# Both branch projections in half products: Strassen units for the first branch, direct halves of the second parked in DRAM

## The chip, the cores and the metric

One core of one Trainium2 chip runs the kernel. The metric is the device time of one execution in microseconds (us), smaller being better. The five engines of the core run side by side, each with its own queue that it works off in order: PE multiplies matrices into PSUM, DVE (VectorE), ACT (ScalarE) and POOL (GpSimd) work element by element, and SP mostly issues DMAs, which move tiles between DRAM and SBUF. ACT issues DMAs too. Semaphores hold an instruction back until what it needs is there.

## The reference, cut to what matters

One layer of a streaming encoder for 1024 prompt rows and 128 sample rows, 1152 rows in all, of width 1024. Two branches make y_m (1152 x 2048) and y_a (1152 x 1024). The change touches only what comes after them:

```python
gate_m = jax.nn.sigmoid(mg_m + b_merge[:D_MODEL])
gate_a = jax.nn.sigmoid(mg_a + b_merge[D_MODEL:])
u = gate_m * jnp.einsum('ble,ed->bld', y_m, w_br_m) + gate_a * jnp.einsum('ble,ed->bld', y_a, w_br_a)
out = jnp.einsum('bld,de->ble', u, w_out)
x_new = layer_norm(DN_ALPHA * x + out, ln_g, ln_b)
```

So there are three products: y_m with w_br_m (2048 rows of weights), y_a with w_br_a (1024), and u with w_out (1024).

## The kernel before, in words

Every float32 number is split into a high part and a low part, and each product is three matmuls: high by high, high by low, low by high. The halving costs an ACT cast (the high part) and a DVE or POOL subtraction (the low part) for every operand. The 1152 columns (tokens) go in three chunks c of 384, which are `ch(0)` to `ch(2)`; the 1024 output channels in eight tiles j of 128. `acc` holds the projected sum, eight tiles by three chunks, in SBUF. `gate_d` in DRAM holds tanh values for the gates, j for the first branch and 8 + j for the second; (1 + tanh) stands for twice the sigmoid, and the factor 0.5 is put into w_out when it is split.

The end of the kernel is a row of stages, each of which keeps PE in one kind of product.

1. `quarter(A0)` multiplies 512 rows of w_br_m directly: four weight tiles, each with two j and three c, four row tiles k, three matmuls each, 288 matmuls. Each result is copied into `acc` by ACT.
2. `unit()` does the middle 1024 rows of w_br_m. For the columns of chunks 0 and 1 it uses Strassen's scheme (in Winograd's form): seven half products in place of eight; chunk 2 is done directly. It goes in four passes p, each for two output tiles j1, j2. A pass has eight weight pieces (B11, B21, B12, B22 and the differences T1 to T4) in an order that `PIECES` gives, and 11 products of 12 matmuls each: 528 in all. `prepare()` makes the piece three places ahead: for a T piece a subtraction first, then an ACT cast and a POOL subtraction. After each product `to()` adds the PSUM result into one to four places of `acc`, on DVE.
3. `quarter(A1)` does the last 512 rows of w_br_m directly; its evacuation `evac_m` adds the result to `acc` and multiplies by the first gate, on DVE.
4. `whole(B1s)` does the second branch, all 1024 rows of w_br_a directly, 576 matmuls. `evac_a` multiplies the result by the second gate on DVE and adds it to `acc` on POOL. Meanwhile `load_wo` loads and splits six of the eight row tiles of w_out; the last two come through the common weight stream (`todo`, `fetch`, `split`).
5. The output product goes chunk by chunk: `acc` is split into u's high and low parts, then 8 row tiles of w_out are multiplied, in chunk 0 with the row tile as the outer loop over six PSUM banks, and a layer norm on DVE follows. Each row tile of chunk 0 is 18 matmuls of 512 columns.

The inputs of the unit (sums and differences of row tiles of y_m) are made in `load_sums` while `quarter(A0)` runs, and the rows of `A1` in `rows_c01` and `rows_c2` while the unit runs. `Flow` meters these generators: a `yield n` gives way for n ticks, and a tick is six matmuls, about 1.04 us.

What sets the order: code inside `with tc.manual_schedule():` (the unit is one such section) goes to each engine's queue as written. Outside, a planner orders the instructions by program order and its own idea of when each becomes ready; `tc.high_priority(6000)`, used for the weight halving in `split()`, moves instructions up there. PSUM has eight banks, taken in turn by `bank()`. Buffers come by tag from pools: a new tile of a tag waits until the old one's readers are done. `wr` has one buffer for a raw weight tile, `wh` and `wl` two each for halves or pieces, `yr` four for row tiles.

## Time and profile before

| | |
|---|---|
| median of 3 runs | 2016.03 us (2015.63 to 2016.05) |
| profiled execution, its own time | 2015.91 us |
| its span, first to last instruction | 2014.1 us |
| PE busy | 2004.5 us of the span |
| DVE busy | 1299.2 us |
| ACT busy | 913.8 us |
| POOL busy | 531.4 us |
| DMA | 292.51 MB, mean 145 GB/s |

The profile page gives busy times of the engines, the chain of work that ended last, and groups of instructions. A group's row has line, engine, operation, out<-in, shape and count, then busy time and mean time of one instruction in ns, then the idle time before them and what ended it. A row of the timeline has start in us, duration in us, engine, line, operation and operands. A row of a windows view has the stretch, its length, busy time and instruction count of PE, weight loading, DVE, ACT and POOL, then the granted PE clock, the busy share of the DMA engines and GB/s. Times in views count from the start of the span. Matmuls overlap in the pipeline: the duration of one is longer than the distance from one start to the next.

### The profile page before, as it was taken

The numbers are of one execution on the slowest core, as the hardware profiler recorded it, in microseconds if no ns is written. First come the engines' busy times: TensorE is split into PE (matmuls) and PEld (weight loads), VectorE is DVE, ScalarE is ACT, GpSimd is POOL, SyncE is SP. The second block draws the span as 40 slices with busy tenths as digits, with TensorE's granted clock in tenths as the row PEclk, the third lists the DMA queues.
The fourth block names the chain that finished last, engine by engine and source line by source line (L and its number), as shares of the span: only waits on it lengthen the run. The fifth ranks groups of instructions, "written<-read, shape, count | busy, mean of one in ns | idle before, by whom it ended". The sixth has DMA issues, their size and how long they took to land.

```text
span 2014.1 us, 36174 instructions
## 1 busy us (share of the span) xinstructions
PE 2004.5 (100%) x14247; PEld 1861.9 (92%) x14247; DVE 1299.2 (65%) x2165; ACT 913.8 (45%) x1971; POOL 531.4 (26%) x708
## 2 busy tenths in 40 slices
PE   9999999999999999999999999999999999999998
PEld 7899999999999999999988988888989899999987
DVE  4145766666667676653577786787776787582355
ACT  4225555554655556543545546455455453221210
POOL 0012445354535354523001001100100005414400
PEclk9999999999999999999999999999999999999999
DMA  7422242424243323243566566566556662274322
GB/s 224 160 74 90 67 145 68 134 79 132 78 126 94 127 78 133 88 143 106 177 216 202 184 209 198 176 208 210 190 198 195 231 231 100 83 234 136 99 90 95
DMA packets 123626, 292.51 MB, mean 145 GB/s; under 512 B 18632, under 2 KB 74944, under 8 KB 113216
## 3 DMA queue, kind: packets, MB, share of 16 engines
q1 hardware_dynamic: 110480, 208.34, 32.3%
q10 hardware_dynamic: 12976, 81.86, 11.9%
q8 instruction: 112, 1.84, 0.4%
q14 instruction: 58, 0.48, 0.1%
HBM read 233.64 MB, written 56.51 MB: 144 GB/s over the span
## 4 chain that ended last, share of the span: by engine, by line
PE 90%; DVE 5%; DMA 2%; ACT 1%; issue 1%; POOL 0%; SPq 0%; ACTq 0%; DVEq 0%; POOLq 0%
PE d L245 19%; PE d L247 18%; PE d L246 18%; PE s L951 3%; PE o L1026 2%; PE y L736 2%; PE dq L245 2%; PE dq L246 2%; PE dq L247 2%; PE out L1614 2%; PE out L1613 2%; PE out L1615 2%; PE v L334 2%; PE v L333 2%; PE v L335 2%; PE so L1101 1%
## 5 line engine op out<-in xcount | busy, mean ns | idle before, releaser
L245 PE MATMUL d<-xh,wh 128*128 128x384 f32 x2112 | 736.1, 349 | 0.0
L247 PE MATMUL d<-xh,wl 128*128 128x384 f32 x2112 | 708.3, 335 | 0.0
L246 PE MATMUL d<-xl,wh 128*128 128x384 f32 x2112 | 707.2, 335 | 0.0
L245 PEld LDWEIGHTS d<-xh,wh 128*128 128x128 f32 x2112 | 396.6, 188 | 19.0 <-issue 8.1
L246 PEld LDWEIGHTS d<-xl,wh 128*128 128x128 f32 x2112 | 397.2, 188 | 0.8
L247 PEld LDWEIGHTS d<-xh,wl 128*128 128x128 f32 x2112 | 396.4, 188 | 0.0
L225 POOL TENSOR_TENSOR wl<-wr,wh 128x1024 fp32r<-128x1024 f32 x45 | 107.8, 2396 | 203.6 <-ACT wh L224 203.4
L956 ACT ACTIVATE st<-s,ckt 128x256 f32<-128x256 f32 (+1 forms) x320 | 115.1, 467 | 18.2 <-PE s L951 16.0
L224 ACT CAST wh<-wr 128x1024 fp32r<-128x1024 f32 x56 | 58.7, 1049 | 120.4 <-PE d L246 93.6
L1016 ACT ACTIVATE st<-st 128x1024 f32<-128x1024 f32 x80 | 83.2, 1062 | 40.9 <-DVE st L1011 38.0
L960 POOL TENSOR_TENSOR st<-st,mask_bf 128x256 f32<-128x256 f32 x64 | 49.7, 797 | 193.7 <-ACT st L956 193.4
L705 ACT ACTIVATE m<-ce,nacum 128x128 f32<-128x128 f32 x288 | 96.9, 392 | 5.7 <-PE y L736 5.7
L228 DVE SCALAR_TENSOR_TENSOR wl<-wr,wh 128x1024 fp32r<-128x1024 f32 x50 | 62.7, 1255 | 32.8 <-ACT wh L227 32.8
L1428 POOL TENSOR_TENSOR pc<-wu,pc 128x512 fp32r<-128x512 f32 x32 | 44.3, 1398 | 124.4 <-ACT pc L1427 124.3
L632 POOL TENSOR_TENSOR wx<-xdt,wdt 128x256 f32<-128x256 f32 x72 | 54.0, 752 | 84.8 <-DVE xdt L630 84.8
L1026 PE MATMUL o<-st,vt 128*64 128x256 f32 (+1 forms) x640 | 68.6, 363 | 0.2
L1026 PEld LDWEIGHTS o<-st,vt 128*64 128x64 f32 x640 | 43.0, 137 | 26.0 <-issue 3.0
L245 PE MATMUL d<-yb1h,wh 128*128 128x384 f32 x192 | 64.1, 334 | 0.0
L246 PE MATMUL d<-yb1l,wh 128*128 128x384 f32 x192 | 64.1, 334 | 0.0
L247 PE MATMUL d<-yb1h,wl 128*128 128x384 f32 x192 | 64.1, 334 | 0.0
L227 ACT ACTIVATE wh<-wr 128x1024 fp32r<-128x1024 f32 x50 | 52.7, 1054 | 22.2 <-PE d L246 22.2
L851 ACT ACTIVATE gate<-d,bcol 128x384 f32<-128x384 f32 x48 | 27.7, 578 | 71.8 <-PE d L247 46.6
(773 smaller groups left out, 4173.3 us busy)
## 6 DMA issues: line engine op xcount, KB each, us to landing
wr<-in_wt SPq DMA_DIRECT2D x88, 512.0 KB
kc<-in_cache_k ACTq DMA_DIRECT2D x32, 1024.0 KB
vc<-in_cache_v ACTq DMA_DIRECT2D x32, 1024.0 KB
ce<-ac_d SPq DMA_DIRECT2D x96, 192.0 KB
sb<-cs_d ACTq DMA_DIRECT2D x16, 576.0 KB
yr<-ym_d SPq DMA_DIRECT2D x16, 576.0 KB
g<-gate_d SPq DMA_DIRECT2D x48, 192.0 KB
gate_d<-gate SPq DMA_DIRECT2D x45, 192.0 KB
```

The source lines that it names most:

```text
L224: ac.copy(hi[:, :cols], raw[:, :cols])
L225: lazy.get("sub", po).tensor_tensor(lo[:, :cols], raw[:, :cols], hi[:, :cols].bitcast(F32), ALU.subtract)
L228: ve.scalar_tensor_tensor(lo[:, :cols], raw[:, :cols], scale, hi[:, :cols].bitcast(F32), ALU.mult, ALU.subtract)
L245: te.matmul(out, wh, xh, start=(k == 0), stop=False)
L246: te.matmul(out, wh, xl, start=False, stop=False)
L247: te.matmul(out, wl, xh, start=False, stop=(k == n - 1))
L632: po.tensor_tensor(wx[b][:], xdt[b][:], wdt[:, b, hs][:, :, None].to_broadcast([P, 4, 64]), ALU.mult)
L705: ac.activation(m[:, j, :], ce[:, j * P:(j + 1) * P], AF.Abs, bias=nacum[:, b, h:h + 1])
L951: te.matmul(ps2[:, e, 256 * x + q0:256 * x + 256], kk[hr, ks], qq[hr, qs], start=(at == 0), stop=(at == 2))
L956: ac.activation(S[j][:, e, kb, q0:], ps2[:, e, 256 * x + q0:256 * x + 256], AF.Identity, bias=ckt[:, kb, 2 * hp + e:2 * hp + e + 1])
L1016: ac.activation(w, w, AF.Exp, scale=-1.0)
L1026: te.matmul(o[64 * e:64 * e + 64, 256 * at + q0:256 * at + 256], vt[:, kb, 64 * e:64 * e + 64], S[j][:, e, kb, q0:256], start=(kb == 0), s ...
```

## The change

The second branch no longer has a stage of its own. Its 1024 rows of weights are cut into two direct halves of 512 rows, and these take the places of the two quarters of the first branch. The first branch is done wholly in two Strassen units of 1024 rows each. The order is: direct half of y_a, unit 0 (row tiles 4 to 11 of y_m), direct half of y_a, unit 1 (row tiles 0 to 3 and 12 to 15).

- The results of the direct halves can't stay in `acc`, which now belongs to the first branch. They go to a new DRAM tile `pa_d`: the first half through `acc` (ACT copies, then an ACT-queue DMA per j), the second through two small `gt` buffers (a copy and a DMA per j and c).
- `load_sums(v)` runs behind each direct half. Half of its S4 sums stay in the row buffer instead of a `gt` tile, and `gt` has two buffers instead of four, with a new tag `s4` of two.
- Unit 0 copies its first result into each place of `acc` with ACT, where all later ones are added by DVE.
- In unit 1 everything that the last two stages did on the way is put between the products, by `steps_1`: `seconds` loads both halves of the second branch and their gate for chunks 0 and 1, adds and gates them (two DVE instructions over 768 columns per j, three DMAs); `final` loads the first gate, `finish` applies it (DVE) and adds the second branch (POOL). For chunk 0 of the last two tiles this comes after piece T4 in pass 3, with the piece order of that pass changed; there, too, u's parts for chunk 0 are made (`parts_of_u`), and `load_wo` loads row tiles of w_out.
- Chunk 2 is finished during the output product by `late`, one j at a time, with four loads per j through the four small buffers.
- The row tiles of w_out are used in the order 0 to 7. Tiles 0 and 1 come from the weight stream: 0 is fetched at the sixth piece of pass 3 and split at the eighth, and the split then fetches tile 1 into the same raw buffer. `split_wo(k)` does tiles 2 to 7.

The diff, cut:

```diff
-    todo += [(I["wbr"][i], None, 1024) for i in range(12, 24)]
+    todo += [(I["wbr"][i], None, 1024) for i in range(12, 16)] + [None]
     todo += [(I["w_out"][k], 0.5, 1024) for k in range(2)]
...
+    ROWS = [range(4, 12), (0, 1, 2, 3, 12, 13, 14, 15)]
...
-            s4.append(mp.tile([P, CW], F32, tag="gt", name=f"s4_{i}", bufs=4))
-            ve.tensor_tensor(s4[i][:], y1[:, c0], y0[:, c0], ALU.subtract)
+            if i < 2:
+                s4[i] = mp.tile([P, CW], F32, tag="s4", name=f"s4_{v}{i}", bufs=2)[:]
+                ve.tensor_tensor(s4[i], y1[:, c0], y0[:, c0], ALU.subtract)
+            else:
+                s4[i] = y1[:, c0]
...
-    PIECES = [("B11", "B21", "B12", "B22", "T1", "T2", "T4", "T3")] + 3 * [("B11", "B21", "T1", "T2", "T4", "B12", "B22", "T3")]
+    ORDERS = (("B11", "B21", "B12", "B22", "T1", "T2", "T4", "T3"), ("B11", "B21", "T1", "T2", "T4", "B12", "B22", "T3"),
+              ("B11", "B21", "T1", "T2", "B12", "B22", "T4", "T3"))
+    PIECES = [ORDERS[i] for i in (0, 1, 1, 1, 0, 1, 1, 2)]
...
         def to(j, c, d):
-            ve.tensor_tensor(acc[:, j, ch(c)], acc[:, j, ch(c)], d, ALU.add)
-
+            a = acc[:, j, ch(c)]
+            if v == 0 and (j, c) not in begun:
+                begun.add((j, c))
+                ac.copy(a, d)
+            else:
+                ve.tensor_tensor(a, a, d, ALU.add)
...
-            for piece in PIECES[p]:
+            for at, piece in enumerate(order):
                 prepare()
                 if p == 3:
-                    if piece == "B12":
+                    if at == 5:
                         fetch()
-                    if piece == "T3":
+                    if at == 7:
                         split()
-                        flow.after(1, rows_c2)
...
+                steps(p, piece)
...
+    def evac_0(j, c, d):
+        ac.copy(acc[:, j, ch(c)], d)
+        if c == 2:
+            ac.dma_start(pa_d[0, j], acc[:, j, :])
...
+    def evac_1(j, c, d):
+        t = mp.tile([P, CW], F32, tag="gt", name=f"pa{j}_{c}", bufs=2)
+        ac.copy(t[:], d)
+        ac.dma_start(pa_d[1, j][:, ch(c)], t[:])
+
+    flow.start(load_sums(1))
+    quarter(A1, evac_1, lambda: unit_first(1))
+    flow.drain()
...
+    def seconds(*ps):
+
+        for j in (j for p in ps for j in (2 * p, 2 * p + 1)):
...
+            sy.dma_start(g, pa_d[0, j][:, 0:2 * CW])
+            sy.dma_start(x, pa_d[1, j][:, 0:2 * CW])
+            sy.dma_start(t, gate_d[8 + j][:, 0:2 * CW])
+            yield 5
+            ve.tensor_tensor(g, g, x, ALU.add)
+            yield 2
+            ve.scalar_tensor_tensor(g, t, 1.0, g, ALU.add, ALU.mult)
+            yield 1
...
+            ve.scalar_tensor_tensor(a, t[:], 1.0, a, ALU.add, ALU.mult)
+            po.tensor_tensor(a, a, G[j][:, ch(c)], ALU.add)
...
+    def late(j):
+
+        x0, x1, ta, tm = (pending.pop(0) for _ in range(4))
+        a = acc[:, j, ch(2)]
+        ve.tensor_tensor(x0, x0, x1, ALU.add)
+        ve.scalar_tensor_tensor(x0, ta, 1.0, x0, ALU.add, ALU.mult)
+        ve.scalar_tensor_tensor(a, tm, 1.0, a, ALU.add, ALU.mult)
+        po.tensor_tensor(a, a, x0, ALU.add)
+        if j < 7:
+            load_late(j + 1)
...
+    def parts_of_u(c, ks):
...
+        for k in ks:
+            ac.copy(h[:, k, :], acc[:, k, ch(c)])
+            ve.tensor_tensor(l[:, k, :], acc[:, k, ch(c)], h[:, k, :].bitcast(F32), ALU.subtract)
...
+    def steps_1(p, piece):
+
+        a, b = 2 * p, 2 * p + 1
+        at = PIECES[4 + p].index(piece)
+        if p:
+            if 1 <= at < 4:
+                finish(1)
+            if at < 4:
+                final(((a - 2, 0), (b - 2, 0), (a - 2, 1), (b - 2, 1))[at])
+            if at == 4:
+                finish(1)
+            if at == 6:
+                finish(len(pending))
+            if at == 7 and p < 3:
+                flow.start(seconds(p + 1))
...
+        if p == 3:
...
+            if at == 5:
+                parts_of_u(0, (5,))
+                flow.drain()
+                final((a, 0), (b, 0))
+            if at == 6:
+                load_wo(4, 5, 6, 7)
+                parts_of_u(0, (6, 7))
+
+    with tc.manual_schedule():
+        sums_last(1)
+        todo.pop(0)
+        flow.start(seconds(0, 1))
+        unit(1, steps_1)
         flow.drain()
...
-    flow.start(load_wo())
-    whole(B1s, evac_a)
-    flow.drain()
...
     last_w = ready.pop(0)
     split()
     wo += [last_w, ready.pop(0)]
-    rows_of_wo = (2, 3, 4, 5, 6, 7, 0, 1)
+    split_wo(2)
+    final((6, 1), (7, 1))
...
+                if k < 5:
+                    split_wo(k + 3)
+                if k == 0:
+                    finish(2)
+                    load_late(0)
+                if k > 1:
+                    late(k - 2)
```

More of the change, by code (lines that the diff above doesn't have):

```diff
@@ L186, in trunk_step @@
     gate_d = dr.tile([16, P, T], F32, name="gate_d")
+    pa_d = dr.tile([2, 8, P, T], F32, name="pa_d")
     v_d = dr.tile([9, P, D], F32, name="v_d")
@@ L1496, in unit_first, with sums_last, part @@
             prepare()
-    flow.start(load_sums())
-    quarter(A0, lambda j, c, d: ac.copy(acc[:, j, ch(c)], d), unit_first)
+    def sums_last(v):
+        prepare()
+        slot["S4"] = (tuple(ap.tile([P, 4, CW], F32R, tag=f"a{x}2", name=f"s4{x}{v}") for x in ("hi", "lo")), 0)
+        for i in range(4):
+            put("S4", i, s4[i])
+    def evac_0(j, c, d):
+        ac.copy(acc[:, j, ch(c)], d)
+        if c == 2:
+            ac.dma_start(pa_d[0, j], acc[:, j, :])
+    flow.start(load_sums(0))
+    quarter(A0, evac_0, lambda: unit_first(0))
     flow.drain()
     lazy["sub"] = po
-    A1 = [(ap.tile([P, 4, CW], F32R, tag=f"ahi{c}", name=f"ya1h{c}"),
-           ap.tile([P, 4, CW], F32R, tag=f"alo{c}", name=f"ya1l{c}")) for c in range(2)]
-    slot["S4"] = ((ap.tile([P, 4, CW], F32R, tag="ahi2", name="s4h"), ap.tile([P, 4, CW], F32R, tag="alo2", name="s4l")), 0)
+    A1 = [tuple(ap.tile([P, 4, CW], F32R, tag=f"a{x}{c}", name=f"ya1{x}{c}") for x in ("hi", "lo")) for c in range(2)]
     ys = []
-    def parted(i, c):
+    def part(i, c):
         h, l = A1[c][0][:, i, :], A1[c][1][:, i, :]
@@ L1523, in rows_c01, with steps_0 @@
             yield 3
     def rows_c2():
-        A1.append((ap.tile([P, 4, CW], F32R, tag="ahi2", name="ya1h2"), ap.tile([P, 4, CW], F32R, tag="alo2", name="ya1l2")))
+        A1.append(tuple(ap.tile([P, 4, CW], F32R, tag=f"a{x}2", name=f"ya1{x}2") for x in ("hi", "lo")))
         for i in range(4):
-            parted(i, 2)
+            part(i, 2)
+    def steps_0(p, piece):
+        if p == 3 and piece == "B22":
+            flow.after(1, rows_c2)
     with tc.manual_schedule():
-        prepare()
@@ new lines, in final, with finish @@
+    def final(*jcs):
+        for j, c in jcs:
+            count[0] += 1
+            t = mp.tile([P, CW], F32, tag=("gt", "s4")[count[0] % 2], name=f"gm{j}_{c}", bufs=2)
+            sy.dma_start(t[:], gate_d[j][:, ch(c)])
+            pending.append((j, c, t))
+    def finish(n):
+        for _ in range(n):
+            j, c, t = pending.pop(0)
+            a = acc[:, j, ch(c)]
+            ve.scalar_tensor_tensor(a, t[:], 1.0, a, ALU.add, ALU.mult)
+            po.tensor_tensor(a, a, G[j][:, ch(c)], ALU.add)
@@ new lines, in load_late @@
+    def load_late(j):
+        for tag, src in (("gt", pa_d[0, j]), ("gt", pa_d[1, j]), ("s4", gate_d[8 + j]), ("s4", gate_d[j])):
+            t = mp.tile([P, CW], F32, tag=tag, name=f"lt{j}", bufs=2)
+            sy.dma_start(t[:], src[:, ch(2)])
+            pending.append(t[:])
+    def late(j):
[7 more added lines that the diff above has]
+            load_late(j + 1)
@@ new lines, in parts_of_u, with load_wo @@
+    def parts_of_u(c, ks):
+        if c not in U:
+            U[c] = tuple(xp.tile([P, 8, CW], F32R, tag=f"x{x}{c % 2}", name=f"u{x}{c}") for x in ("hi", "lo"))
+        h, l = U[c]
+        for k in ks:
+            ac.copy(h[:, k, :], acc[:, k, ch(c)])
+            ve.tensor_tensor(l[:, k, :], acc[:, k, ch(c)], h[:, k, :].bitcast(F32), ALU.subtract)
+    def load_wo(*ks):
+        for k in ks:
+            pool, tag = {2: (ap, "ahi1"), 3: (ap, "alo1"), 4: (ap, "ahi0"), 5: (ap, "alo0")}.get(k, (mp, "yr"))
+            wraw[k] = pool.tile([P, 1024], F32, tag=tag, name=f"wor{k}", bufs=1 if k < 6 else 4)
+            sy.dma_start(wraw[k][:], I["w_out"][k])
```

200 lines of the change are left out of this document (89 added, 111 removed).

## The prediction

> **What bounds the kernel now.** The first page comes first: the span, the engines, the chain that ended last. PE is busy throughout, and the chain is PE for 90%.
>
> ```profile
> span 2014.1 us, 36174 instructions
> ...
> PE 2004.5 (100%) x14247; PEld 1861.9 (92%) x14247; DVE 1299.2 (65%) x2165; ACT 913.8 (45%) x1971; POOL 531.4 (26%) x708
> ...
> PE 90%; DVE 5%; DMA 2%; ACT 1%; issue 1%; POOL 0%; SPq 0%; ACTq 0%; DVEq 0%; POOLq 0%
> ```
>
> Busy PE may still hide waits, so PE's timeline comes next, at the two borders that matter. Starts lie 0.17 us apart for 384 columns and 0.23 us for 512, and neither border, from the unit to the quarter or from the whole second branch to the output product, shows a gap.
>
> ```profile
> 1758.36 0.34 PE L1442 MATMUL u3m<-S3h,pc 128*128 128x384 f32 x1
> 1758.54 0.34 PE L245 MATMUL dq<-ya1h,wh 128*128 128x384 f32 x1
> ...
> 1908.12 0.33 PE L247 MATMUL d<-yb1h,wl 128*128 128x384 f32 x1
> 1908.30 0.39 PE L1613 MATMUL out<-woh,uh 128*128 128x512 f32 x1
> 1908.53 0.40 PE L1614 MATMUL out<-wol,uh 128*128 128x512 f32 x1
> ```
>
> With these borders a view by stretches has one row per stage (quarter, unit, quarter, whole, output product, and two pieces of the end). PE is busy for all of each of the first five: this end of the kernel costs its matmuls and nothing else, until the last 7.3 us.
>
> ```profile
> 1616.78:1666.70 49.92, 49.92 (x290) 49.92 (x289) 41.90 (x63) 28.88 (x62) 3.17 (x2) 1.00 0.63 211
> 1666.70:1758.54 91.84, 91.84 (x530) 91.84 (x530) 58.79 (x96) 26.13 (x48) 48.90 (x35) 1.00 0.28 94
> 1758.54:1808.46 49.92, 49.92 (x290) 49.92 (x289) 44.75 (x75) 15.89 (x31) 9.67 (x4) 1.00 0.68 224
> 1808.46:1908.30 99.84, 99.84 (x578) 99.84 (x577) 30.44 (x46) 21.10 (x29) 42.47 (x30) 1.00 0.38 118
> 1908.30:2006.77 98.47, 98.47 (x480) 83.46 (x480) 53.15 (x99) 8.43 (x19) 3.67 (x2) 1.00 0.28 102
> 2006.77:2009.64 2.87, 0.28 (x3) 0.08 (x1) 2.45 (x6) 0.29 (x1) 0.00 (x0) 1.00 0.00 0
> 2009.64:2014.10 4.46, 0.00 (x0) 0.00 (x0) 1.46 (x3) 0.00 (x0) 0.00 (x0) 0.50 0.31 118
> ```
>
> **The gain.** The whole stage (576 matmuls, 99.84 us) becomes a second unit (528, 91.84 us): 8.0 us less. Both direct halves keep a quarter's 49.92 us. 8.0 us is 0.40%; differences below 0.2% (4 us) can't be told from none here.
>
> **What must now hide.** The whole stage ran beside 30 us of DVE work; its gating, u's halves and the w_out loads move into unit 1. What each costs there:
>
> ```profile
> L1449 DVE TENSOR_TENSOR acc<-acc,u1m 128x384 f32<-128x384 f32 x14 | 7.0, 547 | 0.2
> L1425 DVE TENSOR_TENSOR wu<-wu,wu 128x512 f32<-128x512 f32 x6 | 4.1, 688 | 4.3 <-POOL pc L1428 2.2 <-DMA wu<-in_wbr 2.0
> L1600 DVE TENSOR_TENSOR ul<-acc,uh 128x384 fp32r<-128x384 f32 x24 | 12.7, 581 | 1.5 <-ACT uh L1599 1.5
> L1552 DVE SCALAR_TENSOR_TENSOR acc<-g,acc 128x384 f32<-128x384 f32 x24 | 16.8, 702 | 0.9 <-DMA g<-gate_d 0.3
> L1563 POOL TENSOR_TENSOR acc<-acc,g 128x384 f32<-128x384 f32 x24 | 29.5, 1228 | 53.3 <-DVE g L1562 53.3
> L1428 POOL TENSOR_TENSOR pc<-wu,pc 128x512 fp32r<-128x512 f32 x32 | 44.3, 1398 | 124.4 <-ACT pc L1427 124.3
> L1599 ACT CAST uh<-acc 128x384 fp32r<-128x384 f32 x24 | 10.4, 509 | 36.1 <-PE out L1614 29.4 <-PE d L247 4.0 <-POOL acc L1563 2.7
> L1578 ACT ACTIVATE woh<-wor 128x1024 fp32r<-128x1024 f32 x6 | 6.4, 1062 | 12.5 <-DMA wor<-in_w_out 12.3
> L1579 DVE SCALAR_TENSOR_TENSOR wol<-wor,woh 128x1024 fp32r<-128x1024 f32 x6 | 8.2, 1362 | 7.5 <-ACT woh L1578 7.4
> ```
>
> In unit 1's last pass DVE has 16 adds, 3 piece differences, 4 instructions of 768 columns for the second branch (estimate: twice 0.55), 6 gatings and 8 low halves. Packed closely, at 0.49 us an add (four took 1.94) and 0.55 for the 384-column others, that is 7.8 + 2.1 + 4.4 + 3.3 + 4.4 = 22 us in a pass of 22.96, where before it had 14.5:
>
> ```profile
> 1735.58:1758.54 22.96, 22.96 (x134) 22.96 (x134) 14.50 (x26) 5.91 (x10) 10.07 (x7) 1.00 0.15 46
> ...
> 1742.28 1.94 DVE L1449 TENSOR_TENSOR acc<-acc,u3m 128x384 f32<-128x384 f32 x4
> ```
>
> **The wait that it adds.** The output product now begins with row tile 0 of w_out, split at the eighth piece. Written before that split are the end of c=0 for tiles 6 and 7: gating (DVE), adding (POOL), u's high half (ACT), low half (DVE). Queues in a hand-ordered section keep the written order: there the weight cast stood behind the evacuation before it, while in a planned stage it had come ahead of that (the last three rows).
>
> ```profile
> 1566.65 0.58 ACT L851 ACTIVATE gate<-d,bcol 128x384 f32<-128x384 f32 x1
> 1567.12 1.05 ACT L227 ACTIVATE wh<-wr 128x1024 fp32r<-128x1024 f32 x1
> ...
> 1629.28 1.05 ACT L224 CAST wh<-wr 128x1024 fp32r<-128x1024 f32 x1 [0.32 <-PE dq L246]
> 1630.24 0.51 ACT L1352 CAST yb0h<-yr 128x384 fp32r<-128x384 f32 x1
> 1630.65 0.47 ACT L1499 COPY acc<-dq 128x384 f32<-128x384 f32 x1
> ```
>
> So behind u's cast of tile 7 stands the scaling of w_out's tile 0, and PE waits for that. Counted from unit 1's last matmul as 0: T4's product ends at -2.09 (12 x 0.174), -1.93 with its pipeline. Its add 0.55, the first gating 0.55, two POOL adds 2 x 1.23, the cast 0.51, the scaling 1.06, the low half 1.36: high part at +3.2, low part at +4.6. PE wants them at 0 and 0.23.
>
> Then tile 1. Its fetch waits until the split has read the one raw buffer; from a fetch to the cast that waited for it took 3.63 us:
>
> ```profile
> 1755.07 0.33 SPq L212 DMA_DIRECT2D wr<-in_wbr  x1
> ...
> 1758.70 1.05 ACT L224 CAST wh<-wr 128x1024 fp32r<-128x1024 f32 x1 [1.57 <-DMA wr<-in_wbr]
> ```
>
> 4.6 + 3.63 + 1.06 + 1.36 = 10.6, where PE without a stall would want tile 1's low part at 18 x 0.228 + 0.23 = 4.3 (98.47 us over 384 matmuls of 512 columns and 96 of 256 are 0.228 for 512). Lateness: 6.3 us, with DVE on time. Tile 2 is loaded long before, and is due 4.1 us later: hidden.
>
> But DVE is not on time. Instructions of DVE between SBUF operands stood still beside POOL: 1.5 us in place of 0.55, twice, and two of the unit's low halves took 2.92.
>
> ```profile
> 1654.99 3.17 POOL L1428 TENSOR_TENSOR pc<-wu,pc 128x512 fp32r<-128x512 f32 x2 [76.63 <-ACT pc L1427]
> ...
> 1655.47 1.53 DVE L1385 TENSOR_TENSOR yr<-yr 128x384 f32<-128x384 f32 x1
> 1657.04 1.53 DVE L1386 TENSOR_TENSOR yr<-yr,yr 128x384 f32<-128x384 f32 x1
> 1658.49 0.55 DVE L1353 TENSOR_TENSOR yb0l<-yr,yb0h 128x384 fp32r<-128x384 f32 x1
> ...
> 1698.76 2.92 DVE L1510 TENSOR_TENSOR ya1l<-yr,ya1h 128x384 fp32r<-128x384 f32 x2 [0.71 <-ACT ya1h L1509]
> ```
>
> From the end of the pass's first four adds' product (-18.8) to -1.4, 17.4 us, DVE has 11.3 us of SBUF work ahead of T4's add (2 differences 1.4, second branch 4.4, 4 gatings 2.2, 6 low halves 3.3), and POOL 4 x 1.40 + 4 x 1.23 = 10.5. If they exclude each other that is 21.8: 4.4 us late, and the second gating waits 0.55 more for POOL. Lateness 11.3. One after the other, without perfect packing, up to 12.5. I take 10.0, nearer this end, because the 2.92 row comes from this very mix of pieces and low halves.
>
> The Trainium skill says the same more strictly ("SBUF — State Buffer", section "SBUF: two separate sides"): a DVE instruction with two SBUF inputs and a POOL instruction lock each other out for whole instructions. The trace agrees (1.53 against 0.55); by it alone the lateness would be the 11.3, and the time 2020.3.
>
> PE's idle time also lowers its clock: the last rows by stretches show 0.50 from 2.87 us after the last matmul. At half speed tile 0's 17 remaining matmuls take 7.7 us, not 3.9; tile 1 comes 6.05 us after tile 0's low part anyway, so 0 to 1.7 more: I take 0.5.
>
> The Trainium skill ("TensorE: Matmul & The Clock Gate", section "What's actually happening") lets the clock rise after about 3.4 us of work; no run here shows a rise, and it would put this term near 0.
>
> **The other parts.** In the first direct half the eight `pa_d` writes are 4.7 MB in 49.92 us, 95 GB/s on 211: the DMA share goes from 0.63 to about 0.91. What that delays is `load_sums`; its last low halves ended at 1665.45 and the product that needs all row tiles of the first was due to finish at 1668.8.
>
> ```profile
> 1663.02 2.43 DVE L1353 TENSOR_TENSOR yb0l<-yr,yb0h 128x384 fp32r<-128x384 f32 x5
> ```
>
> In the second half each copy on ACT waits for the `gt` write two before, and the casts of `load_sums(1)` queue behind it. Two evacuations are 4.16 us apart, less the copy; a 192 KB write should not exceed the 3.63 us of 512 KB. Together 0 to 3 us: I take 0.5. At nothing I cost unit 0's ACT copies (ACT 26 of 92 us there; without that cover 24 x 0.48), the missing scaling of A1's rows (DVE had room), the S4 sums in place, the order of w_out. Chunk 2's work in `late` is 8 x (3 DVE instructions and a POOL add) beside 288 x 0.228 = 66 us of chunks 0 and 1.
>
> **The sum.** Profiled execution 2015.91 - 8.0 + 10.0 + 0.5 + 0.5 = 2018.9; the median of the runs is 0.1 above it: 2019.0. With the lateness from 6.3 to 12.5 and the other unknowns from 0 to 2, this case alone reaches 2014.3 to 2022.5.
>
> **Rivals.** *The split comes early* (the section doesn't hold it back). For: at cross-section borders weight casts did come ahead. Against: the rows at 1566.65. Then tile 0 is ready before 0, and only tile 1 is late, behind 2 MB of w_out that are loading: 1 to 5 us. 2015.9 - 8.0 + 3 = 2011; with tile 1 on time too, 2008.
>
> *Chunk 2 becomes the chain* (slower). `late` reuses four buffers: loads for j + 1 wait for j. A period is 0.55 + 0.70 + 0.70 + 1.23, four issues of 0.33 and up to 3.6 until landing, 8.1 us; eight from about +13 end at +78. The output product wants chunk 2 at 10 + 66 = +76, and u's halves of it take 1.1 more: 3 us, and as much again if DVE, standing at a `late`, evacuates chunk 0 late. 2019 + 3 to 6: 2023.5. For: in-order DVE. Against: landing may be quicker. It decides once a period exceeds 7.7 us.
>
> *Nothing is late*, DVE and POOL fit: 2008, held within the first rival.
>
> **How the numbers follow.** Forecast 0.55 (0.38 within 0.2%, 0.17 slower), early split 0.20 (faster), chunk 2's chain 0.25 (slower). Faster 0.20, same 0.38, slower 0.42. Range 2010.5 to 2025: the early split's middle to the slow rival with the clock term in full.
>
> **What would show it.** 528 matmuls in each unit at 22.96 us a pass; a PE gap of 4 to 10 us before the first output matmul, ended by ACT or DVE on w_out's tile 0, and one of some 2 us at tile 1, ended by the fetch; a granted clock of 0.5 there. Wrong if the split's scaling stands ahead of u's last casts on ACT, if PE waits inside unit 1, or if chunk 2's first matmul waits for `late`.

## The result and the profile after

The changed kernel takes 2039.93 us (median of four runs, 2038.8 to 2040.02) beside 2015.83 us of the kernel before on the same chip: a ratio of 1.0119, 95% interval 1.0102 to 1.0137. The forecast was 2019.0 us with a range to 2025: the direction of the forecast (slower) is right, the size is off by 21 us, and the time lies 15 us above the range. The profiled execution of the changed kernel took 2038.8 us.

The page of the changed kernel: its span, its engines, and its chain of work by engine, of which PE had 90% before.

```profile
span 2037.0 us, 36365 instructions
...
PE 2007.6 (99%) x14199; PEld 1858.2 (91%) x14199; DVE 1351.3 (66%) x2233; ACT 949.2 (47%) x2055; POOL 557.8 (27%) x732
...
PE 80%; DVE 9%; DMA 6%; ACT 2%; issue 1%; POOL 1%; SPq 0%; ACTq 0%; DVEq 0%; POOLq 0%
```

The view by stretches of the same execution (length; busy time and count of PE, weight loading, DVE, ACT, POOL; granted clock; DMA share; GB/s): unit 0, the second direct half, the four passes of unit 1, the wait ahead of the output product, its start, the whole of it.

```profile
1666.93:1758.77 91.84, 91.84 (x529) 91.84 (x529) 39.87 (x66) 36.87 (x75) 47.49 (x35) 1.00 0.25 85
1758.77:1813.80 55.03, 52.04 (x289) 51.40 (x289) 44.66 (x62) 26.93 (x56) 10.44 (x5) 0.97 0.73 239
1813.80:1839.37 25.57, 24.07 (x133) 22.72 (x133) 17.79 (x27) 8.71 (x17) 9.31 (x8) 1.00 0.41 125
1839.37:1866.28 26.91, 23.94 (x133) 22.84 (x133) 18.14 (x28) 4.72 (x9) 17.22 (x14) 1.00 0.49 169
1866.28:1889.58 23.30, 23.25 (x134) 22.92 (x133) 17.60 (x28) 4.78 (x8) 14.03 (x11) 1.00 0.59 212
1889.58:1915.65 26.07, 23.75 (x133) 22.65 (x132) 23.51 (x31) 8.19 (x17) 16.65 (x13) 1.00 0.59 205
1915.65:1922.33 6.68, 0.17 (x1) 0.00 (x1) 6.68 (x12) 2.03 (x4) 2.51 (x2) 0.82 0.84 317
1922.33:1926.50 4.17, 4.17 (x10) 3.34 (x11) 4.17 (x6) 4.17 (x5) 0.00 (x0) 0.50 0.42 125
1922.33:2029.71 107.38, 103.86 (x480) 86.90 (x480) 76.12 (x136) 15.38 (x27) 15.32 (x10) 0.95 0.46 152
```

Without a stall these are 91.84, 49.92, four times 22.96 and 98.47 us. The losses are 5.11 in the second half, 2.61 + 3.95 + 0.34 + 3.11 = 10.0 in unit 1, 6.68 ahead of the output product and 8.91 in it: 30.7 us. Less the 8.0 that the second unit saves, that is the 22.9 between the spans (2037.0 and 2014.1), to 0.2.

*Second half.* ACT's copies of the results wait for `gt` (timeline of the changed kernel; the releaser stands in brackets). The write issued at 1784.00 releases the copy at 1789.58, 5.6 us later; the longest such stretch in this stage is 7.0 us (a write issued at 1768.95, its copy at 1775.93). Behind that copy and the one at 1794.75 stands the cast of the fourth weight tile, and PE waits for the cast, then for the low half. The rows show the clock as well: after 1.18 and 1.81 us of waiting a matmul takes 0.52 us instead of 0.33.

```profile
1784.00 0.81 ACTq L1552 DMA_DIRECT2D pa_d<-pa  x2
1789.58 0.48 ACT L1551 COPY pa<-dq 128x384 f32<-128x384 f32 x1 [2.69 <-DMA pa_d<-pa]
1794.75 0.48 ACT L1551 COPY pa<-dq 128x384 f32<-128x384 f32 x1 [2.42 <-DMA pa_d<-pa]
1796.46 1.04 ACT L225 CAST wh<-wr 128x1024 fp32r<-128x1024 f32 x1
1797.56 0.44 PE L246 MATMUL dq<-ya1hi,wh 128*128 128x384 f32 x1 [1.18 <-ACT wh L225]
...
1799.99 0.44 PE L248 MATMUL dq<-ya1hi,wl 128*128 128x384 f32 x1 [1.81 <-POOL wl L226]
1801.01 0.52 PE L246 MATMUL dq<-ya1hi,wh 128*128 128x384 f32 x1
```

*Unit 1, pass 1.* Three casts of pieces are done on ACT by 1852.3. The low half of one starts on POOL at 1855.11 only, because an add of the second branch (L1590) stands ahead of it; the next low half waits in the same way, behind an add whose gating on DVE waits for its load. PE waits for both low halves.

```profile
1850.61 1.66 ACT L1415 CAST pc<-wu 128x512 fp32r<-128x512 f32 x3 [2.73 <-DVE wu L1413]
1853.49 1.66 POOL L1590 TENSOR_TENSOR acc<-acc,pa 128x384 f32<-128x384 f32 x1 [0.49 <-DVE acc L1589]
1855.11 1.26 POOL L1416 TENSOR_TENSOR pc<-wu,pc 128x512 fp32r<-128x512 f32 x1
1856.42 0.44 PE L1430 MATMUL u11d<-ym1h,pc 128*128 128x384 f32 x1 [1.02 <-POOL pc L1416]
1857.30 0.56 DVE L1589 SCALAR_TENSOR_TENSOR acc<-gm,acc 128x384 f32<-128x384 f32 x1 [2.09 <-DMA gm<-gate_d]
1857.94 1.01 POOL L1590 TENSOR_TENSOR acc<-acc,pa 128x384 f32<-128x384 f32 x1 [1.57 <-DVE acc L1589]
1858.91 1.26 POOL L1416 TENSOR_TENSOR pc<-wu,pc 128x512 fp32r<-128x512 f32 x1
1860.22 0.44 PE L1430 MATMUL u11d<-ym1h,pc 128*128 128x384 f32 x1 [1.42 <-POOL pc L1416]
```

*Start of the output product.* This is the predicted chain: POOL's adds, u's cast of tile 7, the scaling of w_out's tile 0 (L228) right behind it, its low half on DVE (L229). PE waits 6.51 us and then runs at half clock (0.63 for a matmul of 512 columns, 0.39 else) to 1926.8, which costs about 2.2 us more (half of the 4.47).

```profile
1918.27 2.51 POOL L1590 TENSOR_TENSOR acc<-acc,pa 128x384 f32<-128x384 f32 x2 [3.22 <-DVE acc L1589]
1920.81 0.51 ACT L1616 CAST uhi<-acc 128x384 fp32r<-128x384 f32 x1 [0.76 <-POOL acc L1590]
1921.23 1.05 ACT L228 ACTIVATE wh<-wr 128x1024 fp32r<-128x1024 f32 x1
1922.33 3.36 PE L1702 MATMUL out<-wh,uhi 128*128 128x512 f32 x7 [6.51 <-ACT wh L228]
1922.52 1.21 DVE L229 SCALAR_TENSOR_TENSOR wl<-wr,wh 128x1024 fp32r<-128x1024 f32 x1
1925.48 0.63 PE L1703 MATMUL out<-wl,uhi 128*128 128x512 f32 x1
```

*Chunk 2.* The last step `late` ends on POOL at 1990.06, the low halves of u on DVE come at 1990.07 to 1995.68 and later, and PE waits for them, 2.90 us at one place, with half clock behind it. The view by stretches shows DVE busy for 40.45 of the 41.79 us around it (1960.37 to 2002.16), and for 7.02 of the 20 us before.

```profile
1989.04 1.02 POOL L1606 TENSOR_TENSOR acc<-acc,lt 128x384 f32<-128x384 f32 x1 [7.38 <-DVE lt L1604]
1990.07 0.55 DVE L1617 TENSOR_TENSOR ulo<-acc,uhi 128x384 fp32r<-128x384 f32 x1
1995.68 1.01 DVE L1617 TENSOR_TENSOR ulo<-acc,uhi 128x384 fp32r<-128x384 f32 x2
1996.27 0.80 PE L1704 MATMUL out<-wohi,ulo 128*128 128x512 f32 x1 [2.90 <-DVE ulo L1617]
```

```profile
1940.00:1960.00 20.00, 20.00 (x90) 16.58 (x89) 7.02 (x14) 0.97 (x3) 4.04 (x4) 1.00 0.56 160
...
1960.37:2002.16 41.79, 38.27 (x156) 30.83 (x155) 40.45 (x78) 5.42 (x13) 4.50 (x4) 0.92 0.55 184
```

### The profile page after: what moved, and what is told of

The parts are those of the page before. It is cut to its first block, busy times and chain, and to the rows that moved or that the text cites. A ratio compares the mean times of both kernels' runs of the same rounds, so it can differ in the third digit from the quotient of the medians.

```text
span 2037.0 us, 36365 instructions
## 1 busy us (share of the span) xinstructions
PE 2007.6 (99%) x14199; PEld 1858.2 (91%) x14199; DVE 1351.3 (66%) x2233; ACT 949.2 (47%) x2055; POOL 557.8 (27%) x732
## 4 chain that ended last, share of the span: by engine, by line
PE 80%; DVE 9%; DMA 6%; ACT 2%; issue 1%; POOL 1%; SPq 0%; ACTq 0%; DVEq 0%; POOLq 0%
PE d L246 17%; PE d L248 16%; PE d L247 16%; PE s L952 3%; PE o L1027 2%; PE y L737 2%; PE v L336 2%; PE v L335 2%; PE v L334 2%; PE so L1102 1%; PE dS L678 1%; PE y L741 1%; PE ss L1080 1%; PE dq L247 1%; PE dq L246 1%
## 5 line engine op out<-in xcount | busy, mean ns | idle before, releaser
L226 POOL TENSOR_TENSOR wl<-wr,wh 128x1024 fp32r<-128x1024 f32 x37 | 89.0, 2404 | 189.1 <-ACT wh L225 189.1
L1416 POOL TENSOR_TENSOR pc<-wu,pc 128x512 fp32r<-128x512 f32 x64 | 87.9, 1381 | 172.8 <-ACT pc L1415 172.8
L1415 ACT CAST pc<-wu 128x512 fp32r<-128x512 f32 x64 | 38.5, 622 | 116.8 <-DVE wu L1413 88.9
L229 DVE SCALAR_TENSOR_TENSOR wl<-wr,wh 128x1024 fp32r<-128x1024 f32 x50 | 62.1, 1242 | 32.5 <-ACT wh L228 32.4
L225 ACT CAST wh<-wr 128x1024 fp32r<-128x1024 f32 x48 | 50.3, 1049 | 53.7 <-PE d L247 43.9
L686 POOL TENSOR_TENSOR S<-S,ea 128x256 f32<-128x256 f32 x56 | 37.8, 674 | 75.9 <-DVE S L687 64.6
L1038 DVE TENSOR_TENSOR st<-st 128x1024 f32<-128x1024 f32 (+1 forms) x40 | 57.4, 1436 | 0.8
L228 ACT ACTIVATE wh<-wr 128x1024 fp32r<-128x1024 f32 x50 | 52.7, 1054 | 10.7 <-PE d L247 10.7
```

Of the source, the lines that this page charges most:

```text
L226: lazy.get("sub", po).tensor_tensor(lo[:, :cols], raw[:, :cols], hi[:, :cols].bitcast(F32), ALU.subtract)
L229: ve.scalar_tensor_tensor(lo[:, :cols], raw[:, :cols], scale, hi[:, :cols].bitcast(F32), ALU.mult, ALU.subtract)
L1038: ve.tensor_tensor(s[:, :, 0:h, :], s[:, :, 0:h, :], s[:, :, 2 * n - h:2 * n, :], ALU.add)
L1416: po.tensor_tensor(t[:, 512:1024], out, t[:, 0:512].bitcast(F32), ALU.subtract)
```

## The experiments

All start from the changed kernel. The table has, from the profiles, the length in us of the second half, of unit 1's passes 0 to 2, of pass 3 with the wait behind it, and of the output product (first to last matmul), and the median of the runs. Stage lengths say more than times here: the second half, untouched in six of these kernels, took 53.5 to 57.4 us in their profiles, and the start of that stage came anywhere from 1757.3 to 1761.2 with nothing changed ahead of it. The kernel before took a median of 2015.55 to 2016.78 us beside the runs of these kernels, so medians of two of them compare to about 1 us.

| kernel | half 2 | pass 0 | pass 1 | pass 2 | pass 3 + wait | output | median |
|---|---|---|---|---|---|---|---|
| without stalls | 49.92 | 22.96 | 22.96 | 22.96 | 22.96 | 98.47 | |
| changed kernel | 55.03 | 25.57 | 26.91 | 23.30 | 32.75 | 107.38 | 2039.93 |
| e1_four_buffers | 49.93 | 26.18 | 27.03 | 23.83 | 32.76 | 107.45 | 2035.42 |
| e1d_more_buffers | 49.92 | 24.21 | 27.28 | 22.97 | 32.75 | 108.48 | 2031.67 |
| e2_split_first | 53.48 | 26.74 | 26.95 | 23.50 | 26.09 | 110.19 | 2035.58 |
| e3_late_first | 55.07 | 25.44 | 26.89 | 23.73 | 32.75 | 109.24 | 2043.17 |
| e4_add_on_dve | 57.03 | 25.47 | 27.38 | 24.39 | 34.29 | 102.06 | 2036.65 |
| e5_lows_on_pool | 56.86 | 25.50 | 26.94 | 23.03 | 32.74 | 101.20 | 2034.41 |
| e6_gates_early | 57.35 | 25.23 | 24.16 | 22.96 | 31.20 | 105.63 | 2034.55 |
| c1_all_places | 49.92 | 23.90 | 24.38 | 22.96 | 26.04 | 105.59 | 2020.72 |
| c2_finish_in_place | 49.92 | 23.30 | 24.05 | 22.96 | 22.96 | 111.25 | 2021.70 |
| c2_order | 49.92 | 23.06 | 23.93 | 22.96 | 22.96 | 101.92 | 2013.11 |
| c3_dve_later | 49.93 | 23.33 | 24.24 | 22.96 | 22.96 | 104.06 | 2016.58 |
| c4_fetch_first | 49.93 | 23.25 | 24.34 | 22.96 | 22.96 | 102.45 | 2012.90 |

**More buffers for the second half.**

```diff
+    spare = lazy["raw"].tile([P, 1024], F32, tag="raw", name="spare", bufs=1)
...
     def evac_1(j, c, d):
-        t = mp.tile([P, CW], F32, tag="gt", name=f"pa{j}_{c}", bufs=2)
+        n = 3 * j + c
+        if n < 18 and n % 4 >= 2:
+            t = spare[:, CW * (n % 2):CW * (n % 2) + CW]
+        else:
+            t = mp.tile([P, CW], F32, tag="gt", name=f"pa{j}_{c}", bufs=2)[:]
...
```

> The second direct half parks its results through four buffers instead of two for its first 18 evacuations (two places in the raw weight buffer that stands empty until the fourth weight tile). Theory: ACT's copies wait for the writes of the two gt buffers to land (4 to 7 us each), and the weight cast of the fourth tile and nine copies that run over into unit 1 are late for that reason alone. Then the second half takes 50 to 51 us (55.03 in the changed kernel), the start of unit 1 loses 2 to 2.6 us less, and the time falls by 5 to 7.5 us, to 2032.5 to 2035. Rival: the DMA engines are full in this stretch (a share of 0.9 and more), so the writes only queue longer and the loads behind them too; the half still takes 54 us or more and the time stays within 2 us of 2039.9.

The half takes 49.93 us: the 5.1 are gone, and the weight cast is in time. The median falls by 4.5 us, just short of what was expected, because pass 0 gained nothing: the last six results still go through the two `gt` buffers. The second version gives three of these six a place in the free row buffer (`more`):

```diff
...
+        elif n >= 18 and n % 2 == 0:
+            t = more[0][:, ch((n - 18) // 2)]
...
```

> As the run with four buffers, and the last six evacuations of the second direct half have three more places, in the row buffer that load_sums has just finished with. With four buffers the half took 49.93 us, but the first weight piece and S4's casts of unit 1 still stood on ACT behind copies that waited 4.89 us for a gt write, and unit 1's first pass lost 3.2 us. Theory: it is these waits that make the first pass slow; then its first product waits no more, the pass loses under 1.2 us, and the time falls by 2 to 3 us against the run with four buffers, to 2032 to 2034. Rival: the pass is slow because DVE has the second branch's adds and gatings between the sums there; then it still loses 3 us and the time stays at 2035.4.

Pass 0 takes 24.21 us in place of 26.18 and the median falls by another 3.75, so both waits are those for the writes; the rival, DVE's new work in pass 0, explains at most the 1.25 left. Pass 0 in the view by stretches of this version:

```profile
1808.60:1832.81 24.21, 23.48 (x134) 22.83 (x133) 17.09 (x26) 7.83 (x16) 9.08 (x7) 1.00 0.45 148
```

What makes a write land late was not varied. While they are on their way SP has loads of 512 and 576 KB out, and the stretch has a DMA share of 0.73. The Trainium skill ("DMA: Bandwidth & Descriptors", section "Issuing engines are not separate DMA queues") says that the queues of SP and ACT run on the same 16 engines and interleave there; the 5.6 us above agree with that, and no run here isolates it.

**Split of w_out first.** The end of chunk 0 for tiles 6 and 7 goes behind the section.

```diff
-            if at == 6:
+            if at == 6 and p < 3:
                 finish(len(pending))
...
-                parts_of_u(0, (6, 7))
...
     split_wo(2)
+    finish(2)
+    parts_of_u(0, (6, 7))
```

> The end of chunk 0 for the last two tiles (gating, adding, u's parts) is written behind the split of row tile 0 of w_out and no longer ahead of it. Theory (the step of the prediction): the split waits only because it stands behind u's casts on ACT and DVE. Then the gap of 6.67 us ahead of the first output matmul falls to under 1 us, the 2 us at half clock behind it go too, tile 1 of w_out is up to 3 us late, and the time falls by 5 to 8.5 us, to 2031.5 to 2035. Rival: chunk 2's chain ends the output product at the same time whatever its start is, because late runs on its own clock behind loads; then the gap at the start goes, the gap ahead of chunk 2 grows by about as much, and the time falls by 0 to 2 us only.

Neither theory holds: the median falls by 4.35 us. The gap ahead of the first matmul is gone, but behind it PE waits 2.85 us for the low half of tile 0, and later 1.61 for that of tile 1. Pass 3 with its wait and the output product together take 3.85 us less. ACT's scaling is done at 1912.99, before PE's need; DVE, busy without a break, reaches the low half at 1916.05 only. So the written order on ACT was one half of the predicted wait, and DVE, late by itself, the other. How much of DVE's lateness is due to POOL, which the prediction gave as the reason, no run isolates. Chunk 2 still waits for a low half of u, 3.22 us at one place.

```profile
1911.93 1.06 ACT L228 ACTIVATE wh<-wr 128x1024 fp32r<-128x1024 f32 x1 [0.70 <-DMA wr<-in_w_out]
1916.05 1.21 DVE L229 SCALAR_TENSOR_TENSOR wl<-wr,wh 128x1024 fp32r<-128x1024 f32 x1
1917.32 0.80 PE L1704 MATMUL out<-wl,uhi 128*128 128x512 f32 x1 [2.85 <-DVE wl L229]
```

**Chunk 2: the steps or the low halves.**

```diff
                 if k > 1:
                     late(k - 2)
+            late(6)
+            late(7)
...
-            if c == 1 and j < 2:
-                late(6 + j)
```

> The last two of the eight steps that finish chunk 2 are written ahead of chunk 0's layer norm instead of behind its first and second block. Theory: their four loads were late because they stood on SP behind the writes of y, which wait for DVE's layer norm; chunk 2's gaps before its first matmuls (0.79 and 3.07 us and some 13 matmuls at half clock, 8 to 9 us in all) go, and the time falls by 6 to 9 us, to 2031 to 2034. Rival: the period of a step (4.85 us, set by the landing of the gate's load) decides, and DVE's layer norm comes later for it, so that PSUM banks come free late: the gaps move to chunk 1 and the time falls by under 3 us.

The theory falls: the last step ends at 1981.1 in place of 1990.1, and the kernel is 3.2 us slower. DVE stood for the steps' loads (1.63 us for one of them), its layer norms came later, and u's low halves stand behind them at 1995.58 and 1999.41; PE waits 3.44 us for one of them and 2.25 for another.

```profile
1979.67 1.46 POOL L1606 TENSOR_TENSOR acc<-acc,lt 128x384 f32<-128x384 f32 x1 [5.23 <-DVE lt L1604]
1995.58 0.50 DVE L1617 TENSOR_TENSOR ulo<-acc,uhi 128x384 fp32r<-128x384 f32 x1
1996.14 0.76 PE L1704 MATMUL out<-wohi,ulo 128*128 128x512 f32 x1 [3.44 <-DVE ulo L1617]
```

The next run leaves the steps where they were and takes the low halves off DVE:

```diff
-            ve.tensor_tensor(l[:, k, :], acc[:, k, ch(c)], h[:, k, :].bitcast(F32), ALU.subtract)
+            (po if c == 2 else ve).tensor_tensor(l[:, k, :], acc[:, k, ch(c)], h[:, k, :].bitcast(F32), ALU.subtract)
```

> u's low halves of chunk 2 (eight subtractions of 384 columns) are done on POOL, which has little to do in the output product, and no longer on DVE; the steps late stay where they are. Moving late(6) and late(7) ahead had made them 8 us earlier and nothing faster, because the low halves then stood on DVE between layer norms at 1995.6 and 1999.4. Theory: what chunk 2 waits for is its low halves on DVE, which is busy without a break from 1960 to 2002 with the layer norms of chunks 0 and 1, late and these halves. Then the gaps of 0.79 and 3.07 us in chunk 2 and the half clock behind them go, and the time falls by 6 to 9 us, to 2031 to 2034. Rival: the last step late itself is what is missing (its result stood at 1990.1); then at least half of the gap stays, because the low half of tile 7 comes only 0.3 us earlier, and the time falls by under 4 us.

PE is busy for all 101.20 us of the output product, with the last step `late` no earlier than before (its POOL add at 1990.72). What is left over 98.47 is the half clock at the start. The median falls by 5.5 us, short of the 6 to 9 expected; in the profile the output product is 6.18 us shorter, and the second half 1.83 longer. The time was lost to DVE's place in the order, not to the steps or their loads.

```profile
1923.22:2024.42 101.20, 101.20 (x479) 85.47 (x480) 74.71 (x128) 15.39 (x27) 25.05 (x18) 0.97 0.49 162
```

**Unit 1: which engine, or which order.**

```diff
             ve.scalar_tensor_tensor(a, t[:], 1.0, a, ALU.add, ALU.mult)
-            po.tensor_tensor(a, a, G[j][:, ch(c)], ALU.add)
+            ve.tensor_tensor(a, a, G[j][:, ch(c)], ALU.add)
```

> The add of the second branch in unit 1 is done on DVE instead of POOL (24 adds, 0.55 us each on DVE, 1.0 to 1.7 on POOL). Theory: the weight pieces' low halves on POOL stood behind these adds, which wait for DVE's gating and that for the gate's load; then pass 1 of unit 1 takes 24 us or less (26.91 in the changed kernel) and pass 3 24.5 or less (26.07), the chain before the output product is 1.4 us shorter, and the time falls by 4 to 6.5 us, to 2033.5 to 2036. Rival: DVE is the bound in unit 1, and 13 us more on it (3.3 in a pass) cost more than POOL's order: the passes stay as long or get longer, and the time is 2039 to 2045.

The theory, as put, falls: pass 1 takes 27.38 us and pass 3 no less than before. POOL's pieces are free of the adds, but now the subtraction of a T piece stands behind them on DVE. An add costs DVE 0.56 us, or 1.53 beside POOL: the add at 1855.51 stood while POOL worked on three pieces (1853.38 to 1858.18), that at 1860.43 had POOL idle. The median fell all the same by 3.3 us. In the profile the output product begins 5.1 us later than in the changed kernel and is 5.3 us shorter, because chunk 2 does not wait: five of its low halves now stand together at 1986.80, ahead of a layer norm. Why the planner's order came out so is not shown.

```profile
1853.38 4.80 POOL L1416 TENSOR_TENSOR pc<-wu,pc 128x512 fp32r<-128x512 f32 x3 [2.06 <-ACT pc L1415]
1855.51 1.53 DVE L1590 TENSOR_TENSOR acc<-acc,pa 128x384 f32<-128x384 f32 x1
...
1860.43 0.56 DVE L1590 TENSOR_TENSOR acc<-acc,pa 128x384 f32<-128x384 f32 x1
...
1864.81 0.45 PE L1428 MATMUL u11m<-S3h,pc 128*128 128x384 f32 x1 [1.42 <-ACT pc L1415]
...
1986.80 2.42 DVE L1617 TENSOR_TENSOR ulo<-acc,uhi 128x384 fp32r<-128x384 f32 x5
```

The other run keeps the engines and changes the order:

```diff
-            if 1 <= at < 4:
-                finish(1)
-            if at < 4:
-                final(((a - 2, 0), (b - 2, 0), (a - 2, 1), (b - 2, 1))[at])
-            if at == 4:
-                finish(1)
+            if at == 0:
+                final((a - 2, 0), (b - 2, 0), (a - 2, 1), (b - 2, 1))
+            if 2 + (p < 3) <= at < 6:
+                finish(1)
```

> The four gate loads of a pass of unit 1 are issued at its first piece, and the gating and adding of each comes two pieces later than before (in pass 3 one piece). Nothing is taken from any engine. Theory: the weight pieces' low halves on POOL stood behind adds that waited for a gating that waited for its load; with the loads earlier the order on POOL costs nothing: pass 1 takes 24 us or less (26.91 in the changed kernel), pass 3 starts without its 1.17 us, and the time falls by 3 to 5 us, to 2035 to 2037. Rival: unit 1 is bound by DVE and POOL keeping each other out, whatever the order; then the stalls only move to other pieces, as they did when the adds were moved to DVE (pass 1 took 27.4 us there), and the time stays within 2 us of 2039.9.

Pass 1 falls to 24.16 us, pass 2 runs without a stall, pass 3 starts without one, and the median falls by 5.4. The same work on the same engines then fits nearly: most of the loss was the order on POOL and the late load, which this run does not part, and not a lack of room (1.20 us of the 3.95 in pass 1 stay). The wait ahead of the output product stays as well, 7.30 us, and one of 2.40 for tile 1 of w_out comes behind it, whose scaling stands behind u's casts on ACT.

**All together, and what the combination turned up.**

> All the edits together: more buffers for the second direct half, u's low halves of chunk 2 on POOL, the gates' loads at the start of a pass, the split of w_out's tile 0 ahead of u's parts of tiles 4 to 7, whose gating and adding are moved behind unit 1 too. Theory: the stalls of the changed kernel are separate waits at separate places, so that what each fix takes away adds up: 5.1 (second half) + 2 (first pass) + 3 to 4 (passes 1 and 3) + 6 to 8.5 (start of the output product) + 6 to 8.5 (chunk 2) of 2039.9, that is 2012 to 2018, and below the kernel before (2016.2) if three of them hold in full. Rival: the end of the kernel is bound by DVE, so that each gain ahead of the output product comes back as a wait of chunk 2 or of a layer norm; then the time is 2024 to 2030.

The edits are those above, with u's parts of tiles 4 and 5 and the finish of their chunk 1 moved behind the section as well. The median falls by 19.2 us, more than any single cause, but 2.7 short of the expected range. Stage by stage the fixes hold (half 49.92, pass 2 22.96, no wait in chunk 2); what is left sits mostly in pass 3, at tile 0 and at tile 1 (1.77 us for its low half). The planner had drawn two of the moved gatings forward into unit 1, ahead of the first adds of pass 3, and DVE stood there:

```profile
1886.67 1.16 DVE L1600 SCALAR_TENSOR_TENSOR acc<-gm,acc 128x384 f32<-128x384 f32 x2 [3.17 <-DMA gm<-gate_d]
...
1908.29 0.50 PE L1709 MATMUL out<-wl,uhi 128*128 128x512 f32 x1 [3.19 <-DVE wl L229]
```

```diff
-            if 3 <= at < (7 if p < 3 else 5):
+            if 3 <= at < 7:
                 finish(1)
...
+            if at == 7:
+                parts_of_u(0, (4, 5))
+                finish(2)
+                parts_of_u(0, (6, 7))
...
     split_wo(2)
-    parts_of_u(0, (4, 5))
-    finish(4)
-    parts_of_u(0, (6, 7))
```

> All the edits together, but the gating and adding of chunk 1 for tiles 4 and 5 stays inside unit 1 (pieces six and seven of the last pass), and u's parts of tiles 4 to 7 with the gating of tiles 6 and 7 stand at the end of the last pass in the written order. In the run before, the planner had drawn those two gatings to the start of the last pass, where DVE stood 3.17 us for their load and was late up to the output product. Theory: that hoisted wait made the 2.55 us of stalls at the last piece and most of the 3.36 us at the low half of w_out's tile 0; without it both fall to under 1 us each, tile 1 (fetched when tile 0 is split) still costs 2 to 4 us, and the time falls by 4 to 6 us against that run, to 2014.5 to 2017. Rival: DVE and POOL are full in the last pass anyway; then the low half of tile 0 is still 2 to 3 us late and the time is 2018.5 to 2020.5.

Half of this came true: pass 3 takes 22.96 us and the wait for tile 0's low half is 1.87. But the time did not fall: 2021.70 us, 1.0031 of the kernel before, beside 1.0019 for the run before, with intervals that overlap. Tile 1 became late by much more than expected: the planner put its split, at 1913.57, behind those of all the other tiles, and PE stood 6.02 us.

```profile
1903.81 0.50 PE L1710 MATMUL out<-wl,uhi 128*128 128x512 f32 x1 [1.87 <-DVE wl L229]
...
1914.66 1.65 PE L1709 MATMUL out<-wh,uhi 128*128 128x512 f32 x3 [6.02 <-ACT wh L228]
```

```diff
...
-    last_w = ready.pop(0)
-    split()
-    wo += [last_w, ready.pop(0)]
-    split_wo(2)
+    wo.append((0, ready.pop(0)))
+    split_wo(2)
+    split_wo(3)
+    split()
+    wo.append((1, ready.pop(0)))
...
```

> As the kernel beside it, and the output product uses the row tiles of w_out in the order 0, 2, 3, 1, 4 to 7: tiles 2 and 3 lie in SBUF long before, tile 1 gets 8 us more. Theory: with that nothing of w_out is late, the output product starts without a gap and keeps full clock, only some 4 us of stalls are left in units and start, and the time is 2010.5 to 2013.5, 3.5 to 6 us below the kernel before (2016.8). Rival: chunk 2's steps then become the end of the chain again, because the output product starts earlier and late does not: a gap of 2 to 4 us ahead of chunk 2 and a time of 2014 to 2017.

2013.11 us beside 2015.78 of the kernel before: a ratio of 0.9986, 95% interval 0.9977 to 0.9994, within the expected range. Units and halves are now nearly without loss (unit 1 takes 92.91 us for 91.84), and the output product loses 3.45, most of it in two waits for DVE, 1.86 us for the low half of tile 0 and 0.60 for that of another tile:

```profile
1905.51 0.50 PE L1711 MATMUL out<-wl,uhi 128*128 128x512 f32 x1 [1.86 <-DVE wl L229]
```

Two more runs moved DVE's work behind these places. In the first, in pass 3:

```diff
-            if 3 <= at < 7:
+            if 3 <= at < (7 if p < 3 else 5):
                 finish(1)
...
             if at == 7:
+                split_wo(2)
                 parts_of_u(0, (4, 5))
-                finish(2)
+                finish(4)
```

> As the combined kernel with the order 0, 2, 3, 1, and in the last pass of unit 1 the two gatings of chunk 1 for tiles 4 and 5 come behind the last piece's adds, the split of w_out's tile 2 ahead of u's parts of tiles 4 to 7 (into the place of S4, free by then). The gap of 2.03 us before the low half of tile 0 stood behind those two gatings on DVE (0.55 and 1.12 us), and tile 2's low half behind 3 us of u's parts and gatings. Theory: DVE's order is what is left; the gap falls to under 1 us, the 0.76 us at tile 2 goes, PE keeps its full clock, and the time is 1.5 to 3.5 us lower, 2009.5 to 2011.5. Rival: what is moved back is missing later (u's parts of tiles 4 to 7 or chunk 1), since DVE has no break until the layer norms; then a gap of 1 to 3 us appears later in the output product and the time stays within 1 us of 2013.1.

The rival came nearer, though neither named the place: the wait for tile 0's low half falls to 0.57 us and the one behind it goes, and a new one of 3.08 appears at tile 1, whose fetch SP issued at 1914.34, behind loads that waited for row buffers. The time is 2016.58 us, 3.5 above the order before it where the rival had 1 at most; the ratio to the kernel before is 1.0003 (0.9994 to 1.0012).

```diff
-                load_wo(4, 5, 6, 7)
+                load_wo(4, 5)
...
                 split_wo(2)
+                load_wo(6, 7)
```

> As the run before (gatings of tiles 4 and 5 behind the last piece), and the loads of w_out's tiles 6 and 7, which wait on SP for row buffers that POOL's adds still read, are written behind the fetch of tile 1 and no longer ahead of it. In the run before, that fetch was issued at 1914.34 behind them, 7.5 us after its buffer was free, and PE stood 3.24 us for tile 1. Theory: the order on SP is all of it; that gap goes, 0.7 us at tile 0 is what is left in the output product, and the time is 2010 to 2012.5. Rival: the bulk loads (x's rows, w_out) that are on their way then make the fetch land late anyway, and what DVE does later shows again; then a gap of over 1.5 us stays and the time is 2013 to 2016.

Between the two: the fetch goes out at 1905.35, 9 us earlier, and the wait at tile 1 falls to 1.14 us, now for its low half, behind u's casts on ACT and another tile's low half on DVE; one of 0.83 us, for a low half of u on POOL, comes in chunk 2. The time is 2012.90 us, 0.9987 of the kernel before (0.9978 to 0.9996). It can't be told from the run with the order 0, 2, 3, 1. Each is 0.13 to 0.14% below the kernel before, less than the 0.2% that the prediction took as the least that can be told, though the intervals end below 1. Of the 8.0 us these two lose 3.45 and 3.98 in the output product, by their profiles, and 1.07 and 1.7 in unit 1.

## Why the prediction was wrong, step by step

- **The gain of 8.0 us** was right: unit 0 takes 91.84 us in the changed kernel, and unit 1 92.91 where its waits are out of the way.
- **The `gt` buffers** were the first step that failed. The bound "a 192 KB write should not exceed the 3.63 us of 512 KB" took the time of one load as a bound for a write in a busier stretch; 5.6 and 7.0 us were measured. The term was 0 to 3, taken as 0.5 for the DMA writes and buffers together; it cost 5.11 in the half and, by the difference of the two buffer runs, another 2 in pass 0, because the copies that run over stand on ACT ahead of unit 1's casts. The step asked what a late evacuation delays and named the casts of `load_sums`; the weight cast behind it was missed.
- **Unit 1 without a stall** was the second, and an omission: the sum 7.8 + 2.1 + 4.4 + 3.3 + 4.4 = 22 in 22.96 counted DVE's room and not whose turn it is on POOL. The exclusion of DVE and POOL was used for the last wait alone. Measured: 10.0 us in unit 1, 7.4 of them in passes 1 to 3. The order alone gave back 5.4 of these (26.91 to 24.16, 23.30 to 22.96, and pass 3 without the wait behind it 26.07 to 23.73).
- **The wait at w_out's split** came where and how it was put, with a size of 6.68 + 2.2 at half clock, for 10.0 + 0.5 predicted. Two parts of the reason are shown: the order on ACT by the run that splits first, DVE's lateness by what remained in it. That POOL makes DVE late is argued from the long rows alone. The second gap at tile 1 did not come in the changed kernel; half clock and the planner's order, which runs the high products of tile 0 first, covered it. It came with the first gap gone (1.61 us for the low half in the run that splits first, 6.02 for the high half in a combined one), and once beside it (2.40 with the gates early).
- **Chunk 2** was a rival at 0.25, and its place was right, its mechanism wrong. It needed steps longer than 7.7 us, set by landing; the first six came 4.8 to 5.4 apart, the last two 14.7 and 8.4, because they stand behind layer norms, and bringing these two forward made nothing faster. What was late were u's low halves on a DVE with layer norms of two chunks. The work of `late` beside the 66 us of chunks 0 and 1 had cover in sum, but not in the last 42 us. It cost 6.7 of the 8.91.
- **The early split**, held at 0.20, did not happen: within the section the written order stood. Drawn forward by the planner was something else, once work was written behind the section.

The sum predicted 11.0 us of losses, and there were 30.7: +7.2 at the buffers (7.7 with all of pass 0, for 0.5), +7.4 in passes 1 to 3, +6.7 in chunk 2, -1.6 at the split. The chances gave most of the weight to one chain and treated the rest as hidden. Of the three others, waits in unit 1 were named among the signs of being wrong, with no price; chunk 2 had a price of 3 to 6 us, but outside the sum; the buffers had 0 to 3, and were not among the signs.

## What to carry to other kernels

Room on an engine is not the same as a place in its queue: when work is moved into a stage, ask for each new instruction what stands behind it in order, and when the thing it waits for comes, DMAs included. A buffer that waits for its write to land needs the landing time of that very stretch, and two buffers on an engine that also casts weights put that time on PE. A wait at the end hides others: tile 1 cost nothing in the changed kernel, 1.61 and 2.40 us in two of the single edits, and 6.02 in a combined kernel.
